# A hybrid Hyena, GLA and MLA step on one core: a smaller first segment in the opening, and x loaded and squared ahead of the vectors

## The chip, the cores and the metric

The kernel runs on one core of one Trainium2 chip. The metric is the device time of one execution in microseconds, as the median over runs. A core has TensorE (PE, with its weight loads shown apart as PEld), VectorE (DVE), ScalarE (ACT), GpSimd (POOL) and SyncE (SP). They run beside each other, each in the order of its own instructions, and wait for each other by semaphores. Loads are issued here from SP's queue (most weights) and from ACT's queue (small vectors, x, constants). Both feed the same 16 DMA engines.

## The reference, cut to what matters

Two groups of 128 tokens (prompt and sample), 2048 features, two layers. Each layer makes six modulation vectors per group from a condition vector, and the first two of them (shift and scale) are needed before the layer's input projection can start:

```python
mod_ctx = jax.nn.silu(c_ctx)[None] @ w_mod[l] + b_mod[l]     # w_mod[l]: 2048 x 12288
mod_lat = jax.nn.silu(c) @ w_mod[l] + b_mod[l]
...
sh1, sc1, g1, sh2, sc2, g2 = [m[:, None] for m in jnp.split(mod, 6, axis=-1)]
h = rms_norm(x, lp['ln_mix']) * (1.0 + sc1) + sh1
u_hy, u_gla, u_mla = _split(h @ lp['w_in'], (HY_IN, GLA_IN, MLA_IN))
...
h = jnp.sin(freq[0] * (z @ w1 + b1))     # hyena_filters: from constants and weights alone
```

## The kernel before, in words

The residual x lies transposed in `xT`: 16 feature tiles (k tiles) of 128 features by 256 tokens. Every large product is a loop over k tiles. For each, `weights` (L300 on) loads a row block of the weight on SP's queue, ACT rounds it to `wh`, DVE makes the remainder `wl`, and `gemm_steps` issues three matmuls per block (`hh,wh`, `hl,wh`, `hh,wl`, all L343) into four banks `pg`. `norm_mod` makes the right operands `hh` and `hl` of one k tile from `xT`, `rstd` and `modv` (four DVE steps, two ACT steps, two DVE steps of 128x128).

The opening, which is all up to the MLA part of layer 0, is cut in segments by `SPLIT = (4, 4, 4, 4)`. For each segment `mod_first(k0, n, ...)` makes shift and scale of n feature tiles: it needs all 2048 rows of `w_mod`, so it loads 16 tiles `mw` (L196, SP's queue, one per k tile, each 128 rows of 2 pieces of 128n floats), multiplies each with the condition `sc` in one step of four fp32 matmuls on 32 columns each (L207), turns the result (`mtr`) and adds `b_mod` and the norm's weight (`mod_put`). A segment then runs the 736 columns of `c_a` (18 matmuls of 256 columns per k tile) and the 1024 columns of `c_gla` (12 of 256 and 6 of 512) over its k tiles, adds the sums of the segments in SBUF (`put`), and has the steps of the next segment's `mod_first` between its own (`MSTEP`). The last segment runs `c_a` in the same way and leaves `c_gla` to fill gaps of the MLA part. From segment `FQ` on, one `hyena_filters` per segment (12 fp32 matmuls of 512 columns, L580 to L589, and two small ones, L558) stands between them.

Ahead of the segments stands the head (`px0`): c is transposed and put through silu (`sc`); the norm weights come in 11 small loads into `rows` and are transposed to `vT`; `b_mod` comes in two loads `rb` through one buffer and is transposed to `bT`; then `mod_first` of segment 0; then 10 small loads `rows2` for the convolution and filter vectors (`v2T`); then x, in four loads `xin` of 512 KB on ACT's queue (L523), 32 transposes (L530), squares on ACT and sums on DVE (`SquareSum`), four matmuls with `ones` (L426) and `rsq` for `rstd`.

What is written here in order is then put in order once more: a scheduler places the instructions of all engines before the run, so that the order on an engine is that of its list and not of the text. Tiles of `mw` use a pool of six buffers (`MP0`), and `w` one of five. A load also waits for the load that took the same one of eight completion semaphores before it, whichever queue that stood on.

Of the kernel before, what the change touches and what calls it, by code (L numbers as in the profile page):

```python
# [10 lines left out]
F32 = mybir.dt.float32  # L11
# [5 lines left out]
D = 2048  # L17
KT = D // 128
# [10 lines left out]

MSTEP = 3  # L30
AHEAD = 4
FQ = 1
SPLIT = (4, 4, 4, 4)
MP0 = 6
MT = 10
MT2 = 14
# [66 lines left out]
def tile_backbone(ctx, tc, T, O):  # L103
    nc = tc.nc
# [5 lines left out]
    def PR(name, bufs=1):  # L110
        return P(name, bufs, side="right")
# [18 lines left out]
    def stt(out, a, s, b, op0, op1):  # L130
        r = nc.vector.scalar_tensor_tensor(out=out, in0=a, scalar=s, in1=b, op0=op0, op1=op1)  # L131
        dve["last"] = r.ins.name
# [12 lines left out]
    def act(out, a, func=AF.Copy, **k):  # L145

        name = table_of.get(func)
        if name is not None and name != table["name"]:
            ld = nc.scalar.preload_act_table_set(name)
            for u in table["users"]:  # L150
                tc.add_manual_dep(ld.ins, u, no_sync, reason="table")
            table.update(name=name, load=ld.ins.name, users=[])
        r = nc.scalar.activation(out=out, in_=a, func=func, **k)  # L153
        if name is not None:
            tc.add_manual_dep(r.ins, table["load"], no_sync, reason="table")
            table["users"].append(r.ins.name)
        return r
# [3 lines left out]
    def px(shape):  # L161
        return ps_x.tile(shape, F32, tag="x", name="px")


    ident = base.tile([128, 128], F32, name="ident")
# [6 lines left out]
    xT = base.tile([128, KT, 256], F32, name="xT")  # L172
# [7 lines left out]
    rstd = base.tile([128, 256], F32, name="rstd")  # L180
# [8 lines left out]
    def quads(w):  # L189
        return w.rearrange("p (k q j) -> p q k j", q=4, j=32)  # L190

    def mod_first(k0, n, pool, ahead):

        def load(kt):
            w = pool.tile([128, 1024], F32, tag="mw", name="mw0")[:, :256 * n].rearrange("p (m c) -> p m c", m=2)
            nc.sync.dma_start(w, T["w_mod"][0, kt * 128:(kt + 1) * 128, 0:2 * D]  # L196
                              .rearrange("p (m c) -> p m c", m=2)[:, :, 128 * k0:128 * (k0 + n)])
            return w.rearrange("p m c -> p (m c)")

        ps = ps_m.tile([128, 64 * n], F32, tag="mod", name="mps")  # L200
        ws = [load(kt) for kt in range(ahead)]
        for kt in range(KT):
            if kt + ahead < KT:
                ws.append(load(kt + ahead))
            wv = quads(ws.pop(0))
            for q in range(4):
                mm(ps[32 * q:32 * q + 32, :], sc[:, kt], wv[:, q], start=(kt == 0), stop=(kt == KT - 1))  # L207
            yield
        tr = mp.tile([128, KT, 32], F32, tag="mtr", name="mtr", bufs=1)
        nc.vector.transpose(out=tr[:, :2 * n], in_=ps.rearrange("p (k j) -> p k j", j=32))  # L210
        mod_put(0, 0, k0, tr[:, 0:n, 0:2])
        mod_put(0, 1, k0, tr[:, n:2 * n, 0:2])
        yield
# [215 lines left out]
    def rsq(out, ss, tmp):  # L429

        act(out, ss, AF.Ln, bias=eps)
        act(out, out, AF.Exp, scale=-0.5)
        stt(tmp, ss, EPS, out, ALU.add, ALU.mult)
        stt(tmp, tmp, -0.5, out, ALU.mult, ALU.mult)
        stt(out, tmp, 1.5, out, ALU.add, ALU.mult)
        dve["evict"] = dve["last"]
# [28 lines left out]
    mp0 = pro.enter_context(PR("mp0", MP0))  # L465
    with PR("px0") as pool:
        rows = pool.tile([128, 128], F32, name="rows")
        nc.sync.dma_start(rows[0:16], r128(T["c_ctx"], 16))
        nc.sync.dma_start(rows[16:32], r128(T["c"][0], 16))
        nc.scalar.dma_start(ident, T["mats"][:, 0])  # L470
        p = px([128, 128])
        nc.tensor.transpose(p[:, :32], rows[:32, :], ident[:32, :32])
        nc.vector.memset(sc, 0.0)
        act(sc[:, :, 0:2], p[:, 0:32].rearrange("p (g k) -> p k g", g=2), AF.Silu)

        at = 32
        for nm in ("ln_mix", "ln_ffn"):
            for l in range(DEPTH):
                nc.scalar.dma_start(rows[at:at + 16], r128(T[nm][l], 16))
                at += 16  # L480
        nc.scalar.dma_start(rows[at:at + 16], r128(T["ln_final"], 16))
        at += 16
        for nm, n in (("mla_q_norm", 3), ("mla_kv_norm", 2), ("gla_norm", 1)):
            for l in range(DEPTH):
                nc.scalar.dma_start(rows[at:at + n], r128(T[nm][l], n))
                at += n
        p = px([128, 128])
        nc.tensor.transpose(p[:, :at], rows[:at, :], ident[:at, :at])
        nc.vector.tensor_copy(out=vT[:, 32:at], in_=p[:, 32:at])

        for l in range(DEPTH):
            rb = pool.tile([128, 128], F32, tag="rb", name="rb")[:96]
            nc.scalar.dma_start(rb, r128(T["b_mod"][l], 96))
            p = px([128, 96])
            nc.tensor.transpose(p, rb, ident[:96, :96])
            nc.vector.tensor_copy(out=bT[:, l].rearrange("p m k -> p (m k)"), in_=p)

        for _ in mod_first(0, SPLIT[0], mp0, AHEAD):
            pass

        rows2 = pool.tile([128, 128], F32, tag="rb", name="rows2")
        nc.vector.memset(rows2, 0.0)
        at = 0
        for l in range(DEPTH):
            nc.scalar.dma_start(rows2[at:at + 36], T["hy_conv_w"][l].rearrange("i (r c) -> (i r) c", c=128))
            at += 36
        for l in range(DEPTH):
            nc.scalar.dma_start(rows2[at:at + 12], r128(T["hy_conv_b"][l], 12))
            at += 12
        for l in range(DEPTH):  # L510
            nc.scalar.dma_start(rows2[at:at + 1, :64], T["hy_filt_b1"][l:l + 1])
            nc.scalar.dma_start(rows2[at + 1:at + 2, :64], T["hy_filt_b2"][l:l + 1])
            nc.scalar.dma_start(rows2[at + 2:at + 4, :64], T["hy_filt_freq"][l])
            at += 4
        p = px([128, 128])
        nc.tensor.transpose(p[:, :at], rows2[:at, :], ident[:at, :at])
        nc.vector.tensor_copy(out=v2T, in_=p[:, :at])

        for half in range(2):
            xs = []  # L520
            for nm in ("x_prompt", "x_sample"):
                xt = pool.tile([128, D // 2], F32, tag="xin", name="xin", bufs=4)
                nc.scalar.dma_start(xt, T[nm][0, :, half * 1024:half * 1024 + 1024])  # L523
                xs.append(xt)
            for k4 in range(2):
                for g in range(2):
                    p = px([128, 4, 128])
                    for j in range(4):
                        k = 4 * k4 + j
                        nc.tensor.transpose(p[:, j], xs[g][:, 128 * k:128 * k + 128], ident)  # L530
                    k = 8 * half + 4 * k4
                    dst = xT[:, k:k + 4, 128 * g:128 * g + 128]
                    if g:
                        act(dst, p)
                    else:
                        nc.vector.tensor_copy(out=dst, in_=p)
        ss = SquareSum(pool)
        for k in range(0, KT, 2):
            ss.add(k, on_pe=(k == KT - 2), last=(k == KT - 2))
        rsq(rstd, ss.ps, ss.acc[:, 0:256])  # L540


    def hyena_filters(pool, l):
# [413 lines left out]
    for l in range(DEPTH):  # L957
        ls, ro, wo, rc, wc = open_layer(l) if l else head
        with ls:
# [72 lines left out]
            if l == 0:  # L1032
                with PR("filt") as filt:
                    k0 = 0
                    for q, n in enumerate(SPLIT[:-1]):
                        stage["first"] = q == 0
                        kts = k_tiles(range(k0, k0 + n))
                        k0 += n
                        mods = mod_first(k0, SPLIT[q + 1], mp0, AHEAD)
                        for c, plan, ev, kw in ((c_a, plan_a, ev_a, {"pre": norm, "pieces": dup}), (c_gla, plan_gla, ev_gla, {})):  # L1040
# [3 lines left out]
                        for _ in mods:  # L1044
                            pass
                        if q == FQ:
                            nc.scalar.dma_start(mats, T["mats"][:, 1:])
                        if FQ <= q < FQ + DEPTH:
                            hyena_filters(filt, q - FQ)
                stage["first"] = False  # L1050
            every = k_tiles(range(KT))
            order = every[0 if l else KT - SPLIT[-1]:]
            gemm(c_a, order, hT, plan_a, ev_a, pre=norm, pieces=dup)
# [56 lines left out]
            ss = SquareSum(sqp)  # L1110
# [12 lines left out]
        with PR(f"ff{l}") as fp:  # L1123
            f0 = 0
            for seg, nkt in enumerate((16, 16, 12)):
# [34 lines left out]
                if last_seg:  # L1160
                    ss = SquareSum(fp, l == DEPTH - 1)
# [51 lines left out]
```

## Time and profile before

| | us |
|---|---|
| median of three runs | 2512.07 |
| the runs | 2506.38 to 2512.3 |
| the profiled execution | 2512.27 |
| its span, first to last instruction | 2510.5 |
| PE busy in the span | 2445.6 (97%) |
| first matmul of the input projection (L343) | 53.17 |
| first eviction of the last segment's `c_a` | 184.77 |

The span lies 1.8 us inside the profiled execution, and that execution is 0.2 us above the median. Times in the text are microseconds from the span's start. The opening is the first 185 us, 7% of the span.

### The profile page before, as it was taken

The page shows a single profiled execution, that of the slowest core. Times are in us where ns is not written, and L with a number is a line of the kernel's source. Part 1 is how long each engine was busy: PE and PEld are TensorE (multiplying, and loading weights), DVE is VectorE, ACT ScalarE, POOL GpSimd, SP SyncE. Part 2 cuts the span into 40 slices and gives each one's busy share as a digit, 9 for nine tenths or more (in the row PEclk, how much of TensorE's full clock was granted, in tenths as well). Part 3 has the DMA queues.
Part 4 walks back from the last instruction along what each step waited for, and adds up shares of the span by engine and source line. Part 5 has one row for each costly group of instructions (what it writes and reads, how often), then busy time and mean ns, then how long its engine had stood idle before and what let it go on. Part 6 is the DMA issues. An engine that isn't in the chain of part 4 may idle for free.

```text
span 2510.5 us, 47020 instructions
## 1 busy us (share of the span) xinstructions
PE 2445.6 (97%) x19621; PEld 2254.7 (90%) x19621; DVE 1693.8 (67%) x2399; ACT 1032.3 (41%) x1405; POOL 0.2 (0%) x4
## 2 busy tenths in 40 slices
PE   6999999999999999999999999999999999999998
PEld 3567777999999999999998887899999999999998
DVE  2665555887879968988878556588684545454455
ACT  2334342454433333434446444335444334433443
POOL 0000000000000000000000000000000000000000
PEclk9999999999999999999999999999999999999998
DMA  8988888767768768777866667686765566555662
GB/s 291 332 297 306 292 298 301 282 221 250 264 224 292 284 228 302 238 258 258 288 227 190 214 240 243 218 298 215 252 234 178 184 185 185 177 186 166 184 204 93
DMA packets 167305, 601.21 MB, mean 239 GB/s; under 512 B 18576, under 2 KB 24882, under 8 KB 146612
## 3 DMA queue, kind: packets, MB, share of 16 engines
q1 hardware_dynamic: 164104, 592.27, 70.4%
q10 hardware_dynamic: 2988, 5.93, 0.7%
q8 instruction: 154, 2.52, 0.4%
q14 instruction: 59, 0.48, 0.1%
HBM read 592.03 MB, written 6.09 MB: 238 GB/s over the span
## 4 chain that ended last, share of the span: by engine, by line
PE 92%; DMA 4%; DVE 2%; ACT 1%; issue 0%; SPq 0%; DVEq 0%; ACTq 0%
PE pg L343 80%; DMA mw<-in_w_mod_dram 4%; PE mps L242 3%; PE px L862 2%; PE mps L207 1%; PE px L922 0%; PE px L426 0%; DVE macc L259 0%; PE px L268 0%; PE px L580 0%; PE px L623 0%; PE px L767 0%; DVE wl L126 0%; PE px L625 0%; PE px L914 0%
## 5 line engine op out<-in xcount | busy, mean ns | idle before, releaser
L126 DVE TENSOR_TENSOR wl<-w,wh 128x1024 fp32r<-128x1024 f32 (+3 forms) x816 | 872.2, 1086 | 547.5 <-ACT wh L153 543.2
L153 ACT ACTIVATE wh<-w 128x1024 fp32r<-128x1024 f32 (+3 forms) x816 | 767.8, 950 | 1140.3 <-PE pg L343 971.0
L343 PE MATMUL pg<-hh,wh 128*128 128x256 f32 x3648 | 1038.8, 286 | 9.9 <-ACT hh L153 9.1
L343 PE MATMUL pg<-hl,wh 128*128 128x256 f32 x3648 | 1035.0, 284 | 0.0
L343 PE MATMUL pg<-hh,wl 128*128 128x256 f32 x3648 | 1032.0, 284 | 2.7 <-DVE wl L126 2.7
L343 PEld LDWEIGHTS pg<-hh,wh 128*128 128x128 f32 x3648 | 688.8, 189 | 46.3 <-issue 26.5
L343 PEld LDWEIGHTS pg<-hl,wh 128*128 128x128 f32 x3648 | 691.4, 190 | 10.6 <-issue 9.1
L343 PEld LDWEIGHTS pg<-hh,wl 128*128 128x128 f32 x3648 | 689.8, 189 | 11.8 <-issue 7.2
L343 PE MATMUL pg<-al,wh 128*128 128x256 f32 x1408 | 396.8, 282 | 0.0
L343 PE MATMUL pg<-ah,wl 128*128 128x256 f32 x1408 | 395.0, 281 | 0.0
L343 PE MATMUL pg<-ah,wh 128*128 128x256 f32 x1408 | 395.0, 282 | 0.0
L259 DVE SCALAR_TENSOR_TENSOR macc<-mw,sc,macc 128x1024 f32<-128x1024 f32 x300 | 370.8, 1280 | 6.6 <-DMA mw<-in_w_mod_dram 6.6
L343 PEld LDWEIGHTS pg<-ah,wh 128*128 128x128 f32 x1408 | 264.6, 188 | 1.7 <-issue 1.7
L343 PEld LDWEIGHTS pg<-ah,wl 128*128 128x128 f32 x1408 | 265.6, 189 | 0.1
L343 PEld LDWEIGHTS pg<-al,wh 128*128 128x128 f32 x1408 | 265.5, 189 | 0.1
L242 PE MATMUL mps<-mw,sc 128*32 128x512 f32 x640 | 88.8, 604 | 10.4 <-DMA mw<-in_w_mod_dram 10.4
L131 DVE SCALAR_TENSOR_TENSOR xT<-pg,modv,xT 128x128 f32<-128x128 f32 x256 | 69.6, 343 | 24.0 <-PE pg L343 24.0
L343 PE MATMUL pg<-ymh,wh 128*128 128x256 f32 x256 | 72.4, 286 | 0.6 <-DVE xT L131 0.6
L343 PE MATMUL pg<-yml,wh 128*128 128x256 f32 x256 | 72.2, 283 | 0.0
L343 PE MATMUL pg<-ymh,wl 128*128 128x256 f32 x256 | 71.6, 283 | 0.0
L207 PE MATMUL mps<-mw,sc 128*32 128x256 f32 x512 | 45.2, 441 | 14.1 <-DMA mw<-in_w_mod_dram 14.1
L343 PEld LDWEIGHTS pg<-ymh,wh 128*128 128x128 f32 x256 | 48.8, 192 | 5.3 <-issue 5.0
(299 smaller groups left out, 1879.2 us busy)
## 6 DMA issues: line engine op xcount, KB each, us to landing
mw<-in_w_mod_dram SPq DMA_DIRECT2D x160, 1024.0 KB
w<-in_w_ffn_in_dram SPq DMA_DIRECT2D x256, 512.0 KB
w<-in_w_ffn_out_dram SPq DMA_DIRECT2D x176, 512.0 KB
w<-in_w_ffn_in_dram SPq DMA_DIRECT2D x128, 384.0 KB
mw<-in_w_mod_dram SPq DMA_DIRECT2D x64, 512.0 KB
w<-in_w_in_dram SPq DMA_DIRECT2D x64, 512.0 KB
w<-in_w_out_dram SPq DMA_DIRECT2D x64, 512.0 KB
w<-in_w_in_dram SPq DMA_DIRECT2D x64, 256.0 KB
```

The source lines that it names most:

```text
L126: r = nc.vector.tensor_tensor(out=out, in0=a, in1=b, op=op)
L131: r = nc.vector.scalar_tensor_tensor(out=out, in0=a, scalar=s, in1=b, op0=op0, op1=op1)
L153: r = nc.scalar.activation(out=out, in_=a, func=func, **k)
L207: mm(ps[32 * q:32 * q + 32, :], sc[:, kt], wv[:, q], start=(kt == 0), stop=(kt == KT - 1))
L242: mm(ps[32 * q:32 * q + 32, :], sc[:, kt], wv[:, q], start=(kt == 0), stop=(kt == KT - 1))
L259: r = nc.vector.scalar_tensor_tensor(out=acc[:, i, cs], in0=w[:, cs], scalar=c, in1=acc[:, i, cs], op0=ALU.mult, op1=ALU.add)
L343: mm(o, lt, rh, start=(ti == 0 and i == 0 and j == 0), stop=(ti == nt - 1 and i == len(ps) - 1 and j == 2))
L862: mm(o, a, b, start=(st and i == 0 and j == 0), stop=(en and i == len(steps) - 1 and j == 2))
```

## The change

`SPLIT` becomes (2, 2, 4, 4, 4): the first four feature tiles are two segments of two, so that there are five segments. `FQ` goes from 1 to 2, so that the filters still start in the segment that has tiles 4 to 7. The loads of x are written ahead of those of the vectors. Transposes, squares and `rstd` are written behind the first step of segment 0's `mod_first` and ahead of its other steps and of `rows2`. What is computed per tile stays as it is.

```diff
-FQ = 1
-SPLIT = (4, 4, 4, 4)
+FQ = 2
+SPLIT = (2, 2, 4, 4, 4)
...
         act(sc[:, :, 0:2], p[:, 0:32].rearrange("p (g k) -> p k g", g=2), AF.Silu)

+        xin = {}
+        for half in range(2):
+            for nm in ("x_prompt", "x_sample"):
+                xt = pool.tile([128, D // 2], F32, tag="xin", name="xin", bufs=4)
+                nc.scalar.dma_start(xt, T[nm][0, :, half * 1024:half * 1024 + 1024])
+                xin[half, nm] = xt
+
         at = 32
...
-        for _ in mod_first(0, SPLIT[0], mp0, AHEAD):
+        first = mod_first(0, SPLIT[0], mp0, AHEAD)
+        next(first)
+        for half in range(2):
+            xs = [xin[half, nm] for nm in ("x_prompt", "x_sample")]
...
+        ss = SquareSum(pool)
+        for k in range(0, KT, 2):
+            ss.add(k, on_pe=(k == KT - 2), last=(k == KT - 2))
+        rsq(rstd, ss.ps, ss.acc[:, 0:256])
+
+        for _ in first:
             pass

         rows2 = pool.tile([128, 128], F32, tag="rb", name="rows2")
...
-        for half in range(2):
-            xs = []
...
-        ss = SquareSum(pool)
-        for k in range(0, KT, 2):
-            ss.add(k, on_pe=(k == KT - 2), last=(k == KT - 2))
-        rsq(rstd, ss.ps, ss.acc[:, 0:256])
```

On ACT, at the head of its list, the kernel before has the loads of the vectors (`rows`, `rb`) ahead of x:

```order
L479 DMA rows<-in_ln_ffn_dram 16x128
L481 DMA rows<-in_ln_final_dram 16x128
L485 DMA rows<-in_mla_q_norm_dram 3x128 x2
L485 DMA rows<-in_mla_kv_norm_dram 2x128 x2
L485 DMA rows<-in_gla_norm_dram 1x128 x2
L493 DMA rb<-in_b_mod_dram 96x128
L523 DMA xin<-in_x_prompt_dram 128x1024
```

The changed kernel has, at the same place on ACT:

```order
L480 DMA xin<-in_x_prompt_dram 128x1024
L153 ACTIVATE sc<-px 128x16x2
L480 DMA xin<-in_x_sample_dram 128x1024
L480 DMA xin<-in_x_prompt_dram 128x1024
L480 DMA xin<-in_x_sample_dram 128x1024
L486 DMA rows<-in_ln_mix_dram 16x128 x2
```

The four loads of x now stand ahead of every vector, and the vectors follow them. The large constants `mats` stand between the two loads of `rb` (behind `rows2` before).

On PE, from the last transposes of x to the first matmul of the projection (`pg<-hh,wh`), the kernel before has three steps of the second segment's `mod_first` (mw_414 to mw_418) behind the square sums (`px<-sqa,ones`):

```order
L530 MATMUL px<-ident,xin 128x128 x3
L207 MATMUL mps<-mw_220,sc 32x256 x4
L426 MATMUL px<-sqa,ones 128x256 x2
L426 MATMUL px<-sq,ones 128x256 x2
L207 MATMUL mps<-mw_414,sc 32x256 x4
L207 MATMUL mps<-mw_416,sc 32x256 x4
L207 MATMUL mps<-mw_418,sc 32x256 x4
L343 MATMUL pg<-hh,wh 128x256 x3
```

In the changed kernel PE has 16 steps of segment 0 and three of segment 1 (up to mw_418) ahead of the transposes of x, and then goes on like this:

```order
L502 MATMUL px<-ident,rb 128x96
L514 MATMUL px<-ident,xin 128x128 x12
L207 MATMUL mps<-mw_418,sc 32x128
L207 MATMUL mps<-mw_420,sc 32x128
L514 MATMUL px<-ident,xin 128x128 x12
```

and the stretch from the square sums to the projection reads:

```order
L207 MATMUL mps<-mw_459,sc 32x128 x4
L426 MATMUL px<-sqa,ones 128x256 x2
L426 MATMUL px<-sq,ones 128x256 x2
L207 MATMUL mps<-mw_522,sc 32x128 x4
L207 MATMUL mps<-mw_528,sc 32x128 x4
L207 MATMUL mps<-mw_534,sc 32x128 x4
L207 MATMUL mps<-mw_540,sc 32x128 x4
L207 MATMUL mps<-mw_546,sc 32x128 x4
L207 MATMUL mps<-mw_552,sc 32x128 x4
L343 MATMUL pg<-hh,wh 128x256
L544 MATMUL px<-ident,rows_336 128x104
L343 MATMUL pg<-hh,wh 128x256 x2
```

All 16 steps of segment 1 (mw_414 to mw_552, half as wide as before) stand ahead of the first matmul of the projection, and the transpose of `rows2` comes right behind it.

On SP, the two `c_gla` weights of segment 0 (`w`, 128x1024) stand ahead of the last six of those loads in the changed kernel; before, they stood behind all 16 of segment 1:

```order
L196 DMA mw_453<-in_w_mod_dram 128x2x256
L305 DMA w<-in_w_in_dram 128x1024
L196 DMA mw_459<-in_w_mod_dram 128x2x256
L305 DMA w<-in_w_in_dram 128x1024
L196 DMA mw_522<-in_w_mod_dram 128x2x256
```

From a point in the MLA part of layer 0 on, PE's list is the same in both kernels to the end.

## Rows read from the trace of the kernel before

**Rows 1.** The page, part 1: busy time of the engines in the span.
```profile
PE 2445.6 (97%) x19621; PEld 2254.7 (90%) x19621; DVE 1693.8 (67%) x2399; ACT 1032.3 (41%) x1405; POOL 0.2 (0%) x4
```

**Rows 2.** Opening by stretches: busy PE, PEld, DVE, ACT, POOL; clock, DMA share, GB/s.
```profile
0.00:3.00 3.00, 0.00 (x0) 0.00 (x0) 1.44 (x10) 1.28 (x1) 0.20 (x4) 1.00 0.19 36
3.00:10.00 7.00, 3.53 (x25) 0.81 (x25) 0.00 (x0) 0.20 (x1) 0.00 (x0) 1.00 0.89 294
10.00:26.00 16.00, 6.26 (x35) 1.79 (x35) 0.91 (x4) 0.00 (x0) 0.00 (x0) 1.00 0.95 328
26.00:33.00 7.00, 5.53 (x39) 1.46 (x43) 0.27 (x1) 1.28 (x1) 0.00 (x0) 1.00 0.74 219
33.00:45.00 12.00, 9.92 (x66) 6.18 (x62) 4.57 (x7) 4.54 (x9) 0.00 (x0) 1.00 1.03 386
45.00:53.17 8.17, 3.91 (x41) 2.12 (x34) 7.10 (x22) 6.89 (x16) 0.00 (x0) 1.00 0.84 299
53.17:57.10 3.93, 3.93 (x19) 3.76 (x20) 3.16 (x13) 1.81 (x6) 0.00 (x0) 0.57 0.93 290
57.10:96.16 39.06, 37.71 (x271) 24.54 (x269) 25.86 (x66) 13.54 (x31) 0.00 (x0) 1.00 0.91 305
96.16:118.00 21.84, 20.04 (x195) 11.56 (x194) 7.99 (x22) 3.20 (x8) 0.00 (x0) 1.00 0.97 362
118.00:125.30 7.30, 6.39 (x27) 5.12 (x23) 7.24 (x22) 4.23 (x8) 0.00 (x0) 0.53 0.78 285
0.00:184.70 184.70, 154.85 (x1107) 97.58 (x1108) 99.00 (x250) 59.14 (x128) 0.20 (x4) 0.97 0.89 305
```

**Rows 3.** The chain that ended last, up to 53.2: start, length, what.
```profile
9.65 13.11 DMA mw<-in_w_mod_dram
...
29.93 7.93 DMA mw<-in_w_mod_dram
...
47.67 2.01 PE px L426 x8
...
53.17 0.38 PE pg L343
```

**Rows 4.** PE's timeline: start, length, what, idle before and releaser.
```profile
14.98 0.42 PE L495 MATMUL px<-ident,rb 96*128 96x96 f32 x1 [2.55 <-DMA rb<-in_b_mod_dram]
...
33.64 2.18 PE L530 MATMUL px<-ident,xin 128*128 128x128 f32 x9
...
44.37 0.55 PE L530 MATMUL px<-ident,xin 128*128 128x128 f32 x3
...
117.22 0.43 PE L558 MATMUL px<-fy,fw 64*64 64x128 f32 x2 [1.80 <-ACT fy L153]
...
121.77 0.58 PE L343 MATMUL pg<-hh,wl 128*128 128x256 f32 x1 [0.91 <-DVE wl L126]
...
167.23 0.39 PE L343 MATMUL pg<-hh,wl 128*128 128x256 f32 x1 [1.76 <-DVE wl L126]
```

**Rows 5.** The chain that ended last, 53 to 187: prices of PE's pieces.
```profile
71.28 0.57 PE mps L207 x8
...
77.97 1.06 PE px L588 x2
...
82.57 13.66 PE pg L343 x90
```

**Rows 6.** DVE's timeline: the first eviction of the last segment's `c_a`.
```profile
184.77 1.14 DVE L126 TENSOR_TENSOR cq<-pg,cq 128x512 f32<-128x512 f32 x2
```

**Rows 7.** Loads issued in the first 120 us: count, KB each.
```profile
mw<-in_w_mod_dram SPq DMA_DIRECT2D x48, 512.0 KB
w<-in_w_in_dram SPq DMA_DIRECT2D x8, 512.0 KB
w<-in_w_in_dram SPq DMA_DIRECT2D x9, 368.0 KB
xin<-in_x_prompt_dram ACTq DMA_DIRECT2D x2, 512.0 KB
...
mats<-in_mats_dram ACTq DMA_DIRECT2D x1, 832.0 KB
```

**Rows 8.** SP's queue on the w_mod stream: us in total, times, longest us.
```profile
SPq L196 <- PE mps L207: 34.1, 20, 8.0
SPq L196 <- DMA mw<-in_w_mod_dram: 25.1, 10, 5.6
```

More of the change, by code (lines that the diff above doesn't have):

```diff
@@ L496, in tile_backbone @@
             nc.vector.tensor_copy(out=bT[:, l].rearrange("p m k -> p (m k)"), in_=p)
-        for _ in mod_first(0, SPLIT[0], mp0, AHEAD):
+        first = mod_first(0, SPLIT[0], mp0, AHEAD)
+        next(first)
+        for half in range(2):
+            xs = [xin[half, nm] for nm in ("x_prompt", "x_sample")]
+            for k4 in range(2):
+                for g in range(2):
+                    p = px([128, 4, 128])
+                    for j in range(4):
+                        k = 4 * k4 + j
+                        nc.tensor.transpose(p[:, j], xs[g][:, 128 * k:128 * k + 128], ident)
+                    k = 8 * half + 4 * k4
+                    dst = xT[:, k:k + 4, 128 * g:128 * g + 128]
+                    if g:
+                        act(dst, p)
+                    else:
+                        nc.vector.tensor_copy(out=dst, in_=p)
+        ss = SquareSum(pool)
[3 more added lines that the diff above has]
+        for _ in first:
             pass
@@ L517, in tile_backbone @@
         nc.vector.tensor_copy(out=v2T, in_=p[:, :at])
-        for half in range(2):
-            xs = []
[L521 to L536, printed above, removed]
-        ss = SquareSum(pool)
-        for k in range(0, KT, 2):
-            ss.add(k, on_pe=(k == KT - 2), last=(k == KT - 2))
-        rsq(rstd, ss.ps, ss.acc[:, 0:256])
     def hyena_filters(pool, l):
```

## The prediction

> **What bounds the kernel now.** I read the page first: PE is busy for 97% of the span [rows 1], so time can only be won where PE waits. The reader is to see next, in the table of stretches [rows 2], that the largest such place is the start. PE is busy for 3.5 of 7 us, 6.3 of 16, 5.5 of 7 up to 33 us, and only from 57.1 on for nearly all of each stretch. The chain of the opening [rows 3] says what it waits for: loads of `w_mod` (13.1 us from 9.65, 7.9 us from 29.93), then, from 47.67, the square sums, `rstd` and the first `hh`, until the first projection matmul at 53.17. The opening thus has two parts: a head limited by loads, then PE's list, which the last segment's `c_a` ends at 184.77 [rows 6].
>
> Is PE really full in the second part? I add up its list with prices from the chain [rows 5]. The 90 pieces in 13.66 us are 66 matmuls of 256 columns and 24 of 512, so 114 units of 256 columns at 0.120 us. A `c_a` tile (18 units) costs 2.16 us, a `c_gla` tile (24 units) 2.88. A `w_mod` step costs 0.57, a filter matmul 1.06; a small filter matmul I put at its 0.43 [rows 4]. Behind 53.17 stand 16 `c_a` tiles (34.6), 12 `c_gla` tiles (34.6), 45 `w_mod` steps (25.7; 16 of segment 0 and 3 of segment 1 are ahead), 24 filter matmuls (25.4) and 4 small ones (1.7): 121.9 us. The list takes 184.77 - 53.17 = 131.6, so 9.7 us are lost. Rows show most of it: waits of 1.80, 0.91 and 1.76 us [rows 4], and a clock near 1.2 instead of 2.4 GHz in two stretches, worth 3.93 x 0.43 = 1.7 and 7.3 x 0.47 = 3.4 us (the second partly inside the waits) [rows 2]. So PE's list bounds this part, and an earlier first matmul moves the end by as much, if loads keep up. The DMA engines are busy for 0.89 of the opening at 305 GB/s, and reach 362 to 386 in some stretches [rows 2]: room for some microseconds, not for twenty.
>
> **The change part by part.** *When the first projection matmul can start.* I count bytes that must land before it, with the KB of [rows 7] and 0.262 MB for each half-wide `w_mod` tile. Halving segment 0 would save 4.2 MB, but PE's new list has all 16 steps of segment 1 ahead of that matmul too: 32 x 0.262 = 8.39 MB, against 19 x 0.524 = 9.96 before. Add x 2.10, two `c_a` weights 0.75, the two `c_gla` weights that SP now issues ahead of the last six tiles 1.05, `mats` 0.85, and 0.25 for `ident`, `b_mod` and vectors (an estimate from their shapes): 13.4 MB. The five stretches to 45 us moved 0.11 + 2.06 + 5.25 + 1.53 + 4.63 = 13.58 MB [rows 2], so at the old rates the last byte comes at 44.5, and with a step and the landing the matmul at 45.5.
>
> *x ahead.* Before, the last x transposes end at 44.9 [rows 4], and squares, sums, `rstd` and `hh` take 8.3 us from there to 53.17. Now the transposes stand behind 19 half steps, so behind 4.98 + 2.10 + 0.75 + 0.85 + 0.25 = 8.9 MB. At the old rates that is 33.0 us. At 386 GB/s from 10 us on it is 27.5. All 32 transposes now run nearly together: 9 took 2.18 us [rows 4], so 32 take 7.4. Adding 8.3 gives 43.2 to 48.7. So the two conditions meet: I take 46.0 for the first matmul, 7.2 us earlier. The bounds are 43.2 from below (bytes at 386 throughout would allow 40) and from above the price of the first slower rival.
>
> *What goes behind the first matmul in PE's list.* 48 `w_mod` steps instead of 45 (+1.7) and the transpose of `rows2` (0.4, as the one of `rb`): 124.0 us. That is 2.1 us given back.
>
> *The vectors behind x.* They are needed for `vT` and `bT`, so for `modv`, which nothing uses before the first `hh`. PE waited 2.55 us for `rb` at 14.98 with the steps queued behind it [rows 4]; now its transpose stands behind 16 steps. The second `rb` is issued behind `mats`, and the x transposes stand behind it on PE. It can cost nothing to 2.55 plus 2.2 us (0.85 MB at 386). Those microseconds delay the transposes alone, and lie inside the 43.2 to 48.7; nothing more is added. The `rows2` loads, now among the squares on ACT, may hold PE at the second projection matmul, from nothing to 1.8 us (the nearest wait on ACT, [rows 4]); I take nothing, as the loads are issued before `rstd`.
>
> *32 half-wide steps.* They cost PE at most 32 x 0.57 = 18.2 us in a head in which it idles more than that. SP issues twice as many loads; its queue waits for PE and for loads there [rows 8], not for its own issue.
>
> *One more segment.* Seven more adds of sums on DVE, about 0.57 each [rows 6], 4 us on an engine that is busy for 99 of 185 us [rows 2]; uncovered, PE would wait for the first of each product, 1.2 us. The new boundary matters more: segment 2's 16 full-wide tiles must land. PE is ready for that boundary at 46.0 + 0.4 + 1.7 (low clock, as before) + 4 x 5.04 + 16 x 0.57 = 77.4. By then 24.4 MB must have landed (16.8 of `w_mod`, x 2.1, nine weights 4.0, `mats` 0.85, about 0.65 of small ones and first filter loads). From 13.6 MB at 46, 10.8 MB take 35 us at 305 GB/s or 30 at 362: 76 to 81.5. So PE waits from nothing to 4.1 us; two filter matmuls and two small ones, 3.0 us, stand in its list just there. A fall of the clock at this place would add up to 3.4. I take 0.5, near the lower end, as the filters cover the mean wait.
>
> **Sum.** -7.2 + 2.1 + 0.5 = -4.6 us. From the profiled execution's 2512.27 this is 2507.7; the median of the runs, 2512.07, lies 0.2 below that execution, the fastest run 5.9. Behind the opening PE's list is the same, and the `w_mod` stream there is tied step by step to PE through two buffers, so I carry the shift to the end unchanged.
>
> A rule speaks against the smaller loads. The Trainium skill, "DMA: Bandwidth & Descriptors", section "Anatomy of one DMA", gives a load a fixed cost of about 2.0 us beside its bytes at 436 GB/s (a fit for loads issued by GpSimd). An estimate by it: a load of 256 KB alone takes 2.6 us, and three in flight carry 303 GB/s; 13.4 MB from 3 us on would then put the first matmul at 48, and the sum at 2510. The 386 GB/s of 33 to 45 us [rows 2] was reached with 512 KB tiles; no row shows the smaller ones.
>
> **The rivals.** *Faster than this*: loads run at 386 GB/s from 10 us on, since x is in flight beside `w_mod` from the start and PE is no longer held by `rb`. The first matmul comes at 43.2 and the boundary costs nothing: -10.0 + 2.1 = -7.9, and if PE also loses less up to the boundary (the 1.7 of low clock, up to 2 us of short waits), as low as 2500.7. For it speaks the stretch from 33 to 45; against it that from 26 to 33, at 219 GB/s beside small loads [rows 2]. I call it 2503.
>
> *No change, as loads limit the first eight feature tiles*: the same 16.8 MB of `w_mod` must land before segment 2, however cut. At 290 GB/s behind 46 us the boundary is reached at 83.2, 5.8 late, 2.8 uncovered, and the clock falls (3.4): -7.2 + 2.1 + 6.2 gives 2513.4. For it speaks the DMA share of 0.91 from 57 to 96; against it the 362 behind that.
>
> *Slower*: half-wide tiles halve what is in flight through six buffers and eight semaphores. If the 8.39 MB of `w_mod` in the head run at 219 GB/s, they take 38.3 us, the other 5 MB 13 at 386, from 3 us: the first matmul at 55.3, so +2.1 + 2.1 + 0.5, 2517.0. It decides from a first matmul behind 50.6 on, and beyond 0.3% only behind 58, at 204 GB/s. Against it: the head had 294 to 328 GB/s up to 26 us with the small loads in it.
>
> **How the numbers follow.** About 0.3% (7.5 us) is what a measurement of this kernel can tell from no change. Chances: the forecast 0.45, faster rival 0.32, no change 0.16, slower 0.07. The faster rival's span straddles 2504.7 and takes some of the forecast's spread with it, so faster by over 0.3% has 0.33; slower by over 0.3% needs the slowest end, 0.05; within 0.3% the rest, 0.62. The range goes from the far end of the faster rival, rounded to 2500.0, to just beyond the no-change case, 2514.0; what lies outside is mostly the slower rival.
>
> **What would show each step.** Right: the first projection matmul between 44 and 48 us; the x transposes in one run from 28 to 33 on; segment 2's first matmul between 79 and 83; the last `c_a` eviction near 180, and the same distance from there to the end (2325.7 us of span) as before. Wrong: a first matmul at 50 or later with a rate near 220 GB/s ahead of it (slower rival); an early start, but PE idle for over 5 us or at the low clock around 80 us (no change); an eviction of the last `c_a` below 177 (faster). A shift that is there at 180 us and gone at 460 would show that the later `w_mod` stream takes it back, which I hold for unlikely.

## The result, and the profile after

The changed kernel takes 2523.44 us (median of five runs, 2518.50 to 2530.70) against 2511.15 us (median of five, 2505.12 to 2512.30): a ratio of 1.0057, 95% interval 1.0042 to 1.0073 (the ratio is taken over the runs; the two medians give 1.0049, or 12.3 us). It is 0.6% slower, where 0.2% faster was forecast, and lies outside the range. The profiled execution is 2523.44 us, its span 2521.7.

The page's part 1 and the first eviction of the last segment's `c_a` on DVE (timeline; [rows 1, 6] of before):

```profile
PE 2450.2 (97%) x19749; PEld 2255.4 (89%) x19749; DVE 1699.1 (67%) x2412; ACT 1033.2 (41%) x1405; POOL 0.2 (0%) x4
...
198.02 0.69 DVE L126 TENSOR_TENSOR cq<-pg,cq 128x512 f32<-128x512 f32 x1 [1.31 <-PE pg L343]
```

The eviction comes 13.25 us later than before, the end of the span 11.2. The loss is in the opening; some 2 us come back behind it. Stretches of the opening, with the columns of [rows 2] (the last three are the clock, the DMA share and GB/s):

```profile
26.00:33.00 7.00, 2.70 (x29) 0.81 (x23) 2.84 (x10) 1.95 (x6) 0.00 (x0) 1.00 1.02 341
33.00:45.00 12.00, 9.01 (x93) 7.14 (x94) 7.40 (x14) 6.99 (x12) 0.00 (x0) 0.98 0.70 226
45.00:51.63 6.63, 5.07 (x57) 3.10 (x55) 2.41 (x8) 2.70 (x6) 0.00 (x0) 0.78 0.70 207
51.63:75.30 23.67, 20.28 (x171) 17.42 (x172) 16.95 (x40) 10.38 (x22) 0.00 (x0) 1.00 1.03 351
75.30:78.70 3.40, 3.40 (x18) 1.86 (x20) 0.35 (x3) 0.00 (x0) 0.00 (x0) 0.51 0.36 131
78.70:88.90 10.20, 8.60 (x94) 4.33 (x86) 5.07 (x13) 0.31 (x1) 0.00 (x0) 1.00 0.91 311
88.90:102.70 13.80, 11.48 (x48) 5.65 (x43) 9.67 (x34) 4.21 (x13) 0.00 (x0) 0.51 0.76 266
102.70:150.30 47.60, 44.79 (x345) 28.84 (x338) 28.36 (x70) 13.41 (x31) 0.00 (x0) 1.00 0.89 306
150.30:160.80 10.50, 10.50 (x31) 3.81 (x32) 3.16 (x6) 3.01 (x6) 0.00 (x0) 0.51 0.99 311
```

The reader is to see two things. From 33 us on the loads run at 226 and 207 GB/s, where before had 386 and 299. And behind the first matmul three stretches, 27.7 us together, have a clock of 0.51, which is the level of 1.2 GHz; 0.49 of them, 13.6 us, are lost (1.1 of that inside a wait of PE). Before lost 5.1 us in two such stretches [rows 2].

PE's timeline (start, length, what; in brackets the idle time ahead and what ended it):

```profile
33.53 2.76 PE L514 MATMUL px<-ident,xin 128*128 128x128 f32 x12
...
44.44 2.04 PE L426 MATMUL px<-sqa,ones 128*128 128x256 f32 x4 [0.98 <-DVE sqa L126]
46.27 1.85 PE L426 MATMUL px<-sq,ones 128*128 128x256 f32 x4
...
50.99 0.43 PE L207 MATMUL mps<-mw,sc 128*32 128x128 f32 x8 [0.98 <-DMA mw<-in_w_mod_dram]
51.63 0.38 PE L343 MATMUL pg<-hh,wh 128*128 128x256 f32 x1 [0.20 <-ACT hh L153]
...
73.64 0.38 PE L343 MATMUL pg<-hh,wh 128*128 128x256 f32 x1 [2.18 <-DVE cq L126]
...
85.02 0.43 PE L564 MATMUL px<-fzt,fw 33*64 33x128 f32 x2
...
87.09 0.64 PE L207 MATMUL mps<-mw,sc 128*32 128x256 f32 x8 [1.07 <-DMA mw<-in_w_mod_dram]
88.26 0.43 PE L564 MATMUL px<-fy,fw 64*64 64x128 f32 x2 [0.53 <-ACT fy L153]
88.62 0.88 PE L207 MATMUL mps<-mw,sc 128*32 128x256 f32 x8
91.82 2.07 PE L586 MATMUL px<-fw,fy 64*128 64x512 f32 x2 [2.32 <-ACT fy L153]
93.82 1.08 PE L207 MATMUL mps<-mw,sc 128*32 128x256 f32 x8
94.83 2.07 PE L586 MATMUL px<-fw,fy 64*128 64x512 f32 x2
96.84 1.01 PE L343 MATMUL pg<-hh,wh 128*128 128x256 f32 x3
...
150.16 1.95 PE L586 MATMUL px<-fw,fy 64*128 64x512 f32 x2 [1.87 <-ACT fy L153]
```

The first projection matmul comes at 51.63, 1.5 us earlier than before, not 7.2. Segment 2's first `c_a` matmul comes at 96.84, where 79 to 83 was forecast. Ahead of it stands a chain: a small matmul at 85.02, a sine on DVE and ACT, a small matmul at 88.26, a second sine, and only at 91.82 the first large filter matmul. From 88.9 on each matmul takes about twice its time: a pair L586 takes 2.07 us, 1.06 at the full clock [rows 5].

### The profile page after: what moved, and what is told of

It is laid out like the page before. It is cut to its first block, busy times and chain, and to the rows that moved or that the text cites. A ratio compares the mean times of both kernels' runs of the same rounds, so it can differ in the third digit from the quotient of the medians.

```text
span 2521.7 us, 47320 instructions
## 1 busy us (share of the span) xinstructions
PE 2450.2 (97%) x19749; PEld 2255.4 (89%) x19749; DVE 1699.1 (67%) x2412; ACT 1033.2 (41%) x1405; POOL 0.2 (0%) x4
## 4 chain that ended last, share of the span: by engine, by line
PE 86%; DMA 2%; DVE 1%; ACT 0%; issue 0%; SPq 0%; DVEq 0%; ACTq 0%
PE pg L343 77%; PE mps L242 2%; DMA mw<-in_w_mod_dram 2%; PE px L868 2%; PE px L268 0%; PE px L928 0%; PE px L426 0%; PE px L773 0%; PE px L629 0%; PE px L631 0%; PE px L725 0%; PE px L920 0%; PE px L742 0%; PE px L761 0%; ACT e L153 0%
## 5 line engine op out<-in xcount | busy, mean ns | idle before, releaser
L343 PEld LDWEIGHTS pg<-hl,wh 128*128 128x128 f32 x3648 | 690.2, 189 | 12.9 <-issue 11.1
L207 PE MATMUL mps<-mw,sc 128*32 128x256 f32 (+1 forms) x640 | 48.3, 394 | 17.6 <-DMA mw<-in_w_mod_dram 16.5
L207 PEld LDWEIGHTS mps<-mw,sc 128*32 128x32 f32 x640 | 16.4, 119 | 46.3 <-DMA mw<-in_w_mod_dram 22.9
```

The lines of the kernel that those rows point to most:

```text
L343: mm(o, lt, rh, start=(ti == 0 and i == 0 and j == 0), stop=(ti == nt - 1 and i == len(ps) - 1 and j == 2))
```

## The experiments

**Theory A**: the boundary into segment 2 is the cost. All of PE's work that stands there waits for the two sines or for loads, so PE waits, its clock falls, and the half clock costs more than the waits. **Rival B**: x in one block holds back vectors and loads. **Rival C**: loads of half size are slower. Ratios are to the kernel before, which ran beside each batch (median 2510.99 to 2512.34); evictions, waits and stretches are those of one profiled execution each. From the last `c_a` eviction to the end of the span these executions take between 2319.9 us (the move of x alone) and 2334.3 us (the sines ahead of the segments), so an eviction and an end need not move alike.

**The two parts of the change, each alone.** The move of x with the old segments:

```diff
-FQ = 2
-SPLIT = (2, 2, 4, 4, 4)
+FQ = 1
+SPLIT = (4, 4, 4, 4)
```

> The move of x alone: x is loaded and squared ahead of the vectors, and the opening keeps one segment of four feature tiles at its head. Theory A (the time is lost at the new boundary between the second and the third segment, where the sine chain of the filters leaves PE without other work and its clock falls): this kernel has no such boundary there, so it stays within 3 us of the kernel before, and the stretch from the first projection matmul to the last c_a eviction is 129 to 134 us as before (131.6). Rival B (the transposes of x in one block hold back the vectors and the w_mod loads behind them, and this is the loss): it is 8 to 12 us slower than before, with the first projection matmul at 60 or later. Rival C (half-size w_mod loads): within 3 us of before, as by A.

And the split with x at its old place (the transposes and squares go back behind `rows2`):

> The split alone: two segments of two tiles at the head, filters of the third segment, and x stays behind the vectors. Theory A (loss at the boundary into the third segment, through the sine chain): 8 to 13 us slower than before, with the clock at half for about 10 us or more between 75 and 105 us and the first c_a matmul of the third segment 10 us or more later than the loads allow. Rival B (the loss is the move of x): within 3 us of before, and the first projection matmul earlier than 53.2 by up to 4 us. Rival C (half-size w_mod loads are slower): the first projection matmul later than 53.2, by 2 us or more, and the loss already there at that point.

The move of x alone: 2512.26 us, ratio 1.0009 (0.9996 to 1.0022), first projection matmul 54.13 and last `c_a` eviction 183.82, 129.7 us apart as A said. The split alone: 2521.62 us, ratio 1.0046 (1.0029 to 1.0062), last `c_a` eviction 191.57. So the split is enough for most of the loss and the move of x has none of its own: B falls as the cause. But A's picture of the place was too narrow, and the split alone loses by another path than the whole change: of its 6.8 us at the last `c_a` eviction 4.0 are there at the first matmul. That came at 57.18, with half the clock from 44.6 to 54.8 behind a wait of 2.92 us for `w_mod`, which is the sign of C (tested by itself below); and at the boundary PE waited 1.21 and 1.15 us for `w_mod` and 1.01 for `hh`, not for a sine (stretch of the split alone, columns as above):

```profile
84.00:104.00 20.00, 16.52 (x125) 9.28 (x124) 10.67 (x41) 3.40 (x10) 0.00 (x0) 0.74 0.83 291
```

**Filters one segment earlier.** `FQ = 1` in the changed kernel:

> The whole change, but the filters are those of the second segment instead of the third. Theory A: the large filter matmuls stand around the boundary into the second or third segment; a part of the low clock stays, as PE has as little other work beside the sine chain; 4 to 14 us slower than before. Rival B (move of x): 2523 as the changed kernel, within 3 us, since x stands where it stood. Rival C (half-size loads): 2523 within 3 us.

2530.39 us, ratio 1.0074 (1.0055 to 1.0094): 7 us worse than the change itself, more than A's range. PE waited for sines at two boundaries now (0.77 and 2.56 us around 88, 1.31 and 1.62 around 128), and the half clock stood behind both, at 91 to 97.7 and 128.4 to 138.7. The place of the chain matters, as A says.

**The sines ahead of the segments.** The first half of `hyena_filters`, up to the second sine, becomes `filter_head`, called for both layers ahead of the segments; the large matmuls stay.

```diff
                 with PR("filt") as filt:
+                    for i in range(DEPTH):
+                        filter_head(filt, i)
                     k0 = 0
```

> The whole change, with the sine chains of both layers' filters (the small 64-row matmuls, the wrap on DVE, the sines on ACT) put ahead of the segments; the large filter matmuls stay where they were. Theory A: the waits of PE for the sine (0.53, 2.32 and 1.87 us) go, and with them most of the half-clock stretches at 88.9 to 102.7 and 150.3 to 160.7; 6 to 11 us faster than the changed kernel, so 2512 to 2518. Theory A in a narrower form (the clock falls because PE does filter work on 64 rows there and not for the waits): the waits go, the low clock stays, 2 to 5 us faster than the changed kernel. Rivals B and C: no faster than the changed kernel by over 2 us, except for the 4.7 us of waits themselves if nothing else takes their place.

2510.52 us, ratio 0.9997 (0.9983 to 1.0010): 12.9 us faster than the changed kernel, as much as the change had lost, and more than A's range. The first matmul is at 52.20, no earlier, and the last `c_a` eviction at 183.11, 14.9 us earlier (the profiled execution, 2519.24, was the slowest of the twelve). The boundary now reads:

```profile
84.00:104.00 20.00, 19.97 (x151) 10.55 (x149) 13.91 (x36) 5.07 (x14) 0.00 (x0) 1.00 1.04 363
```

PE is busy for 19.97 of 20 us at the full clock, with the large filter matmuls of 64 rows among the steps. The narrow form of A, that this work itself lets the clock fall, is out.

**The same in the kernel before.**

> The kernel before, with both layers' sine chains put ahead of the segments (large filter matmuls where they were). Theory A (the sine chain costs what it stops: waits of PE and the fall of the clock behind them): before loses to it only the wait of 1.80 us at 117.22 and the half clock from 118 to 125.3 (3.4 us), so 2 to 5 us faster than before, 2507 to 2510; the first projection matmul stays at 52 to 55. Rival (the early chain is itself worth 13 us, whatever the boundary): 2498 to 2501.

2505.63 us, ratio 0.9976 (0.9965 to 0.9986): 5.4 us faster than before, a little more than A said. So the early chain is worth 5 us there and 13 in the changed kernel: some 7.5 of the 12.3 us of loss hang on where the split puts the chain. The other 5 or so us stay between the two kernels even when both have the sines early, and no run takes them apart.

**Wait or clock?** Unused matmuls on 64 rows fill the time in which DVE and ACT make the sines:

```diff
             ts(k, k, 12582912.0, ALU.subtract)
+            pd = px([128, HC])
+            for j in range(2):
+                mm(pd, k, xT[:64, 2 * j:2 * j + 2], start=True, stop=True)
```

> The changed kernel with work added that computes nothing that is used: two 64-row matmuls of 512 columns (about 1.06 us each at the full clock) behind the rounding step of each of the four sine stages, so that PE is busy while DVE and ACT work out the sine; 8 matmuls, 8.5 us of PE more. Theory A with the clock (the cost of a wait here is mostly the half clock that follows): the stretches at half clock from 88.9 to 102.7 and from 150.3 to 160.7 go or shrink to under 5 us each, and although PE has 8.5 us more to do the kernel is 4 to 10 us faster than the changed one, 2513 to 2519. Theory A with the waits alone, or rivals that place the loss elsewhere: no faster, and up to 4 us slower than the changed kernel, 2522 to 2528, with the half clock still there.

2522.66 us, ratio 1.0039 (1.0024 to 1.0054). The half clock at both places was gone, and the last `c_a` eviction came at 190.16, 7.9 us earlier in spite of 8.5 us more of PE; but at the end only 0.8 us were left, so the expected gain was missed there. Behind the eviction this execution takes 9.7 us more than that of the changed kernel; its clock is 0.98 in the stretches from 200 to 300 and from 400 to 500 us (1.00 in both of the changed kernel), which is part of that; the rest stays open. With `range(1)`, half the filling:

> The changed kernel with one unused 64-row matmul of 512 columns behind the rounding step of each of the four sine stages (4.2 us of PE more, about as much as the waits that they fill). If the half clock behind the waits is most of the cost: it goes or shrinks by half or more at 88.9 to 102.7 and 150.3 to 160.7, the last c_a eviction comes at 186 to 191 (198.0 in the changed kernel), and the kernel is 4 to 9 us faster than the changed one, 2514 to 2519. If the clock falls anyhow, because the filter work on 64 rows and the 32-column steps around it don't keep it up: the half clock stays, 2521 to 2525.

2512.68 us, ratio 1.0006 (0.9996 to 1.0016): four matmuls of no use make the changed kernel 10.8 us faster, beyond the expected range. PE's timeline and the stretch of the second chain:

```profile
85.95 1.12 PE L575 MATMUL px<-xT,fk 64*128 64x512 f32 x2 [0.69 <-DVE fk L136]
...
89.26 1.12 PE L575 MATMUL px<-xT,fk 64*128 64x512 f32 x2 [0.69 <-DVE fk L136]
91.13 2.07 PE L589 MATMUL px<-fw,fy 64*128 64x512 f32 x2 [0.75 <-ACT fy L153]
```

```profile
145.00:165.00 20.00, 19.31 (x134) 9.51 (x134) 8.98 (x24) 4.93 (x11) 0.00 (x0) 1.00 0.98 336
```

At the second chain the clock stays at 1.00 (0.74 in the changed kernel over these 20 us); at the first, waits of 0.69, 0.69 and 0.75 us were left, and it still fell from 91 to about 101; with the double filling, waits of 0.69 and 0.98 us were left there and it did not. The last `c_a` eviction is at 192.19. The list of PE from the first projection matmul to that eviction, with the sum of the waits in PE's timeline and the mean clock, reads in the six kernels:

| kernel | list, us | PE's waits, us | mean clock |
|---|---|---|---|
| before | 131.60 | 5.8 | 0.96 |
| changed | 146.39 | 10.6 | 0.91 |
| changed, half the filling | 139.68 | 6.3 | 0.95 |
| changed, all the filling | 137.28 | 5.5 | 0.99 |
| changed, early sines | 130.91 | 6.2 | 0.97 |
| before, early sines | 124.10 | 3.4 | 1.00 |

With half the filling the waits are 4.3 us shorter, and four matmuls, 4.2 us, stand in their place; so the 6.7 us by which the list is shorter are those of the clock. The rows agree: the half clock stands over 13.6 us there (74.1 to 77.5 and 91.2 to 101.4) against 27.7, and 0.49 of the difference is 6.9. So the clock by itself costs several microseconds, apart from the waits. The eviction moved by 5.8 us, as the first matmul came 0.9 later; the rest of the 10.8 us at the end came behind it and stays open.

**The head.** Two buffers for the rows of vectors (`bufs=2` on `rb` and `rows2`):

> The changed kernel with two buffers for the rows of vectors, so that the second load of b_mod does not wait for the first transpose. Theory (the x transposes start at 33.5 because they stand on PE behind the transpose of that second load, and as one block they then hold the w_mod steps): they start 4 us earlier or more, at 29 or before, the half clock at 44 to 48 goes, and the first projection matmul comes at 47 to 50 instead of 51.6. Rival (the w_mod loads alone set the first matmul): it stays at 51 to 52.

The x transposes start at 27.1 (33.5 without) and the first matmul comes at 49.45, as expected, though the half clock did not go (39.5 to 42.9 and 46.3 to 53.1); the one run took 2521.72 us. From 33 to 45 us the loads still ran at 226 GB/s, and PE waited for `w_mod` (1.79, 1.92, 0.63 and 1.10 us). Then the kernel before with `w_mod` in halves:

```diff
-            nc.sync.dma_start(w, T["w_mod"][0, kt * 128:(kt + 1) * 128, 0:2 * D]
-                              .rearrange("p (m c) -> p m c", m=2)[:, :, 128 * k0:128 * (k0 + n)])
+            src = T["w_mod"][0, kt * 128:(kt + 1) * 128, 0:2 * D].rearrange("p (m c) -> p m c", m=2)
+            for c0 in range(0, 128 * n, 256) if k0 == 0 else (0,):
+                c1 = c0 + 256 if k0 == 0 else 128 * n
+                nc.sync.dma_start(w[:, :, c0:c1], src[:, :, 128 * k0 + c0:128 * k0 + c1])
```

> The kernel before with each of the first segment's 16 w_mod tiles loaded as two DMAs of 256 KB in place of one of 512 KB, nothing else changed. If small loads are slower (the slower rival of the prediction): under 270 GB/s from 10 to 33 us and the first projection matmul at 56 or later. If they are not (the x move and the order on PE set the head): within 1.5 us of 53.2, and 295 GB/s or more from 10 to 33 us.

First matmul 53.87, 322 and 220 GB/s from 10 to 26 and 26 to 33 us (328 and 219 before, [rows 2]; over both 291, a little under the 295 expected): half-size loads cost 0.7 us there, and C falls as far as the size of a load goes. What the six buffers hold was not halved here, as it is with half-wide tiles. The one run ended at 2515.18 us, which by itself is no verdict. In the changed kernel, `AHEAD = 5`:

> The changed kernel with five w_mod tiles loaded ahead in place of four, in the same six buffers. If the 226 GB/s between 33 and 45 us is for want of loads in flight (half-wide tiles carry half the bytes each): over 250 GB/s there and the first projection matmul 1 us earlier or more, at 50.6 or before. If it is the order on PE and SP (loads wait for steps that stand behind the x transposes): under 240 GB/s and the first matmul within 0.7 us of 51.6.

189 GB/s from 33 to 45 us and the first matmul at 53.15: one more tile in flight did not help. The rate fits the second outcome, the order on PE and SP; that the matmul came 1.5 us later neither foresaw. The one run took 2529.02 us. What SP waits for in the changed kernel between 26 and 52 us (total, times, longest):

```profile
SPq L196 <- PE mps L207: 7.1, 5, 4.5
SPq L196 <- DMA mw<-in_w_mod_dram: 4.1, 2, 3.3
SPq L196 <- DMA mats<-in_mats_dram: 2.9, 1, 2.9
SPq L196 <- DMA rb<-in_b_mod_dram: 1.6, 1, 1.6
...
SPq L196 <- DMA rows<-in_hy_conv_b_dram: 0.8, 1, 0.8
```

The longest part is PE's steps, which free the buffers of `mw`; the rest are earlier loads, among them `mats` and the small loads of the vectors, with which SP's loads share completion semaphores. In the move of x alone one such wait is 4.4 us. `rows2` was therefore put ahead of `rb`, in a buffer of its own:

> The changed kernel with the ten small loads rows2 written ahead of the two of b_mod, in a buffer of their own, so that none stands among the squares on ACT. If these late small loads hold the w_mod stream through the shared completion semaphores: over 290 GB/s from 33 to 45 us (226 in the changed kernel) and the first projection matmul at 46 to 49.5; the boundary into segment 2 still loses its clock, so the end moves by 2 to 5 us, 2518 to 2522. If the w_mod stream waits for PE's steps behind the block of x transposes: under 250 GB/s and the first matmul at 51 or later.

The rate from 33 to 45 us rose to 337 GB/s, but from 26 to 33 it fell to 210 (341 in the changed kernel): the hole goes where the small loads go, and there SP waits 4.4 us for one of them (`hy_conv_w`). The x transposes, behind the second `rb` on PE, started at 37.5 instead, the first matmul came at 57.52, and the end at 2522.22 us, ratio 1.0041 (1.0026 to 1.0056). So the small loads hold the stream for a part of the time, but that alone does not set the first matmul. How much of the hole in the changed kernel is theirs and how much PE's steps, this run doesn't separate, as both moved.

**Versions that could beat both.** The move of x, two `rb` buffers and the early sines, with the old segments and, as a twin, with the split:

> The move of x, two buffers for the rows of vectors and the early sine chains, with the kernel before's segments (4, 4, 4, 4) and its place of the filters. Theory A: the early chain is worth about 5 us here as it was for the kernel before (2505.6 against 2511.0), the move of x nothing, the second buffer at most 2: 2503 to 2507. Rival (the split brings the expected head start once its new boundary is clean): this one is 3 us or more slower than its twin with the split.

> The whole change with two buffers for the rows of vectors and the early sine chains. Theory A: 2510.5 of the early chain less the 2.2 us by which the second buffer moved the first projection matmul (49.45 against 51.63): 2507 to 2510, so no faster than its twin without the split. Rival (the split's head start is real and was only hidden by the boundary): first projection matmul at 47 to 49.5 and 2499 to 2504.

With the old segments 2503.55 us, ratio 0.9965 (0.9953 to 0.9978), the fastest of all kernels here; with the split 2510.12, ratio 0.9990 (0.9978 to 1.0002). First matmuls 49.85 and 53.57, last evictions 175.09 and 181.88. Even with a clean boundary the split brings no head start, and its kernel is 6.6 us slower than the twin. That its first matmul comes at 53.57, where 49.45 came with two buffers alone, was not expected. Stretches of the fastest kernel:

```profile
33.00:45.00 12.00, 5.92 (x70) 2.90 (x62) 7.17 (x17) 6.92 (x12) 0.00 (x0) 1.00 0.71 228
...
84.00:104.00 20.00, 20.00 (x177) 14.96 (x176) 9.59 (x26) 6.01 (x18) 0.00 (x0) 1.00 0.98 342
```

From 50 to 190 us its clock never falls. The stream still has its hole at 228 GB/s, and SP's waits from 28 to 47 us are:

```profile
SPq L196 <- PE mps L207: 6.6, 2, 5.8
SPq L196 <- DMA rows<-in_hy_conv_b_dram: 4.4, 1, 4.4
```

Both are there again, PE's steps and a small load. So `rows2` was moved in it as well (with one `rb` buffer):

> The same early place of the small loads rows2 (and one buffer for b_mod) in the kernel with the move of x, the early sine chains and segments of four tiles, whose PE waited 4.66 us for w_mod at 46.09. If the small loads hold the stream: that wait falls under 2 us, the first projection matmul comes at 46 to 48.5 (49.85 without), and the kernel is 1 to 4 us faster, 2499.5 to 2502.5. If not: 2503 to 2507.

2510.42 us, ratio 0.9989 (0.9977 to 1.0001), first matmul 57.85: the wait for `w_mod` at 46 went and 381 GB/s flowed from 33 to 45, but PE now waited 3.63 us for `w_mod` at 38.35, and x came late, as above. The expectation fell.

## Why the prediction was wrong, point by point

*What bounds the kernel: right.* PE's list bounds the opening. The 13.25 us at the last `c_a` split into -1.5 at the first matmul and +14.8 in the list behind it (198.02 - 51.63 = 146.4 against 131.6).

*The step that failed is the new boundary*, "I take 0.5, near the lower end, as the filters cover the mean wait". The filter work stands there, but it was no cover: it waits itself, for two sines in a row. Of the 14.8 us, 2.1 are the steps and the transpose that the text counted; 12.7 were set at 0.5. The rows give them. Over PE's busy time the low clock costs 12.4 us against 4.7 before (13.6 and 5.1 over the whole stretches, a part of which are waits), so 7.7; and PE's waits behind the first matmul, 10.6 us in all (0.76, 2.18, 0.32, 1.07, 0.53, 2.32, 0.86, 1.87, 0.37 and 0.33) against 5.8 (0.78, 0.55, 1.80, 0.91 and 1.76), so 4.8; together 12.5. Most of it stands at three places: the boundary into segment 2 (waits of 1.07, 0.53 and 2.32 us, clock 5.6), the chain of the second layer (1.87 and 5.1), and the sums of the added segment at 73.64 (2.18, 0.32 and 1.7).

The trace of before had shown the sign: the wait of 1.80 us for a sine at 117.22, and the low clock from 118 to 125.3 behind it [rows 2, 4]. The text booked that pair as a loss that stays as it is. It did not ask which work of before hid the first layer's sines (the matmuls of segment 0, with waits of 0.55 us at most) and where that cover goes. The early sines show the larger part of the cause: the changed kernel gains 12.9 us by them and the kernel before 5.4, so some 7.5 us are the chain in its new place. About 5 us of the loss remain with the split when the sines are early, and their cause stays open. That the clock costs beside the waits is shown by the filling.

The price that the text gave to a fall of the clock there, 3.4 us, was the right kind of term at half its size: the stretch took 13.8 us of half clock (6.8 lost, 1.1 of it inside a wait), and a second one came at 150.3 (5.1 lost).

*The first matmul: mechanism right, size wrong.* 46.0 was forecast, 51.63 came. The x transposes started at 33.53, beyond the forecast's 27.5 to 33.0, since the second `rb` stood ahead of them: the 4.8 us that the text put inside its bounds. They took 6.6 us (7.4 forecast). From there to the first matmul it was 11.5 us instead of 8.3: the sums ran at the half clock (3.6 us from 44.44 on for the eight instructions L426, 2.0 before, [rows 3]), and the last steps of segment 1 came behind them, waiting for `w_mod`. The rate was the other error: the text carried 305 to 386 GB/s on, and 207 to 226 came, as SP waited for PE's steps behind the block of x and for loads that had been moved, which the text had looked at for PE alone.

*Half-wide steps and tiles: right as far as tried.* The loads of half size cost 0.7 us in the kernel before, where the buffers hold as many bytes as ever. The Trainium skill, "DMA: Bandwidth & Descriptors", section "Anatomy of one DMA", would have made them slower; the estimate was 303 GB/s with three in flight. From 10 to 26 us the trace has 322 with halves, with more than three issued ahead, and 304 in the changed kernel, beside the loads of x. No run has just three such loads in flight, so the estimate is neither borne out nor refuted. *One more segment*: the waits for sums were 2.18 us at 73.64 and 0.32 (1.2 forecast as the uncovered price, nothing taken), with a stretch of half clock behind them; the 2.18 has a second cause, `wl` ahead of the eviction on DVE, and neither was tried by itself.

*The carried shift: nearly right.* From the last `c_a` eviction to the end of the span it was 2323.7 us against 2325.7. The executions profiled here range over 14.4 us in this, so two of them can't tell 2 us from nothing: that it came so near is in part luck.

*The rivals.* "Faster" fell with the rate of 226 GB/s. "No change, as loads limit the first eight tiles" had the right place, but the wrong releaser and size. The slower rival named the right result and the condition under which it decides (a first matmul behind 50.6), and its sign, a rate near 220 GB/s ahead of that matmul, came too. Its mechanism is not borne out: halved loads nearly kept their rate and one more tile in flight did not help. Nor is the first matmul where the time was lost, as it still came 1.5 us earlier than before. With the measured terms the sum reads -1.5 + 2.1 + 12.7 - 2.0 = +11.3 us, on 2512.27: 2523.6. Against the forecast's -4.6 that is 15.9 us, of which PE's waits and half clock behind the first matmul are 12.2, the first matmul 5.7, and -2.0 the end.

## What to carry to other kernels

Work that is to cover a wait must be able to run then: follow its own chain back (here two rounds of small matmul, DVE and ACT) before booking it as cover, and put a long chain with little PE work ahead of a stage or among its matmuls, not at a boundary. When a wait on PE appears in a tuned kernel, price the half clock behind it too; here it cost more than the wait. When loads are moved ahead, list every load that moves back, and what shares a queue or a completion semaphore with it.

## What the runs showed of the hardware

In the changed kernel the clock stayed at 1.2 GHz from 88.9 to 102.7 us. From 91.82 on PE was busy nearly throughout in it, first with filter matmuls on 64 rows and steps of 32 columns, then mostly with full 128x128 matmuls. With the sines early the same filter matmuls ran at 2.4 GHz, and the clock stayed there (1.00 from 84 to 104 us). The fall at 88.9 came behind two waits of 1.07 and 0.53 us. The Trainium skill, "TensorE: Matmul & The Clock Gate", section "HAM oscillation — how this bites in real kernels", prices a cold stretch at its length times one minus the ratio of the clocks, the way the 13.6 us above are worked out. Taking stretches away agreed: with half the filling 14.1 us less of half clock made the list 6.7 us shorter, where waits and filling cancel.

A load on one queue can be held by a small load on another: SP's loads of `w_mod` waited up to 4.4 us at a time for small loads that stood on ACT's queue, with which they share completion semaphores.
